# Pinning the loads of a background matrix-vector product in program order, and splitting eight stored operands at their reload instead of at their store

## The chip, the cores and the metric

The kernel runs on one core of one Trainium2 chip. The metric is the device time of one execution in microseconds. Three runs of the kernel before took 2257.85, 2253.43 and 2251.84 us, a median of 2253.43 us.

## What is computed

One layer of a decoder trunk on a sequence of 1024 tokens with 1024 channels, all in float32. Cut to what matters here:

```
mod = silu(c) @ w_ada + b_ada                       # 1024 -> 6 * 1024
shift1, scale1, gate1, shift2, scale2, gate2 = split(mod)
u = x * (1 + scale1) + shift1
hq, hf, hi, hg, rq, rk, rv, rg, ga, gb = split(u @ w_in)      # 1024 -> 12288
ya = hgrn2(hq, hf, hi, hg) @ w_pa
yb = retention(rq, rk, rv, rg, positions) @ w_pb              # rq, rk are rotated
y  = (sigmoid(ga) * ya + sigmoid(gb) * yb) @ w_o
x  = layer_norm(alpha * x + (1 + gate1) * y)
u  = x * (1 + scale2) + shift2
h  = square(relu(u @ w_up + b_up))                            # 1024 -> 4096
y  = h @ w_down + b_down
x  = layer_norm(alpha * x + (1 + gate2) * y)
```

Two pieces of this are touched: the part of `mod` that is not needed at once (gate2, gate1, scale2, shift2), and the operands made from `h` on their way from the up projection to the down projection.

## The kernel before

**Matrix products.** Each float32 operand is split in two parts, a rounded high part made by ScalarE (line 174) and the rest made by VectorE (line 175), and each product of 128 x 512 outputs is three matmuls (lines 179 to 181). Most of the big projections are done in 2 x 2 blocks with seven products in place of eight: a group of 256 output channels has the seven products A11, S1, S2, S4, S3, A12 and A22, each of 12 matmuls. S1 to S4 are sums and differences of weight blocks that VectorE makes (line 225) from two raw pieces of the weights; the pieces are loaded through SyncE's DMA queue (line 322, 512 KB each, four buffers), and split parts of weights have six buffers. `seven` (line 441) runs the groups. In each group VectorE adds three pairs of results out of PSUM (line 450). The product A22 of a group writes on into the PSUM bank X that the last of these adds has read, so TensorE can't begin it before that add is done.

**Where the order comes from.** The code is a trace in program order. A planner then orders the instructions of each engine by its own estimate of when each is ready, so an instruction with nothing to wait for can go far ahead of its place in the trace. The engines then run their streams in that order, and an instruction that waits holds up all behind it on its engine or queue. `keep_in_program_order` sets an edge from the instruction that was traced last on the same engine, so the pinned one comes after that one; the ones behind it stay free.

**The modulation in the background.** 24 groups of `w_in` (the gates hg, ga and rg, and rq and rk) are computed by `seven` in about 317 to 790 us. Beside the groups that are not rq or rk, the generator `ada_rest` (line 1192) does the rest of `mod` on VectorE: 64 parts of 256 rows by 256 columns of `w_ada`. Each part is one load of 256 KB on SyncE's queue (line 1202, tag adw, four buffers) and two steps on VectorE (lines 582 and 583). After four parts the column sum over the 128 partitions is finished by `ada_row` (line 1227): a load of the bias (line 1233), a split of the sum (lines 1234 and 1236), two small matmuls (lines 1239 and 1240), an add (line 1243) and a store. Before the change the load of part n + 2 was traced behind the steps of part n, nothing but the first step of a part and two VectorE instructions of `ada_row` was pinned, and the planner could issue a load as soon as one of the four buffers was free.

In a group with modulation the calls fall behind the products S1, S4 and A22. The first eight groups take 1, 2 and 2 parts at these places, the eight rg groups 1, 1 and 2. The rg groups alternate with rq and rk groups, which take none; there VectorE has twelve instructions of the rotation to do (lines 731 to 736).

**The operands of h.** For each of 16 groups j of the up projection, `use_square` (line 1527) makes seven operands (L11, L12, L22, S1, S2, S3, S4) that the down projection multiplies, and `keep_h` (line 1516) stores each in DRAM through GpSimd's queue. For the pairs (j, name) in `H_PARTS`, which are L22 and S3 of the groups 0 to 13, it first splits the operand in two parts and stores both (256 KB each). In `down_seven` (line 1572) such a pair is loaded as two parts through GpSimd's queue (line 1593); every other operand comes as one tile through SyncE's queue (line 1596, tag hr, four buffers) and is split then, beside the matmuls. Group 0 is computed by `up_plain` (line 1558), groups 1 to 15 by `seven`. The stages of the down projection run in the order L12 with L11, S1 with S2, S4, S3, L22.

Of the kernel before, what the change touches and what calls it, by code (L numbers as in the profile page):

```python
# [19 lines left out]
P = 128  # L20
T = 1024
D = 1024  # L22
# [4 lines left out]
FT = DFF // P  # L27
# [24 lines left out]

H_DEFER = 4

H_PARTS = [(j, name) for j in range(FT // 2 - 2) for name in ("L22", "S3")]


H_FILL = (0, 4, 3, 0, 3, 0, 2, 0, 1, 0, 2, 0, 1)
# [47 lines left out]
def drain(g):  # L106
    for _ in g:
        pass
# [20 lines left out]
class Trunk:  # L129
# [1062 lines left out]
    def ada_rest(self):  # L1192

        ap = self.aw
        parts = [(s, g, q) for s, g in ADA_ORDER for q in range(4)]
        loaded = {}

        def load(n):
            s, g, q = parts[n]
            c0 = s * D + 256 * g  # L1200
            t = loaded[n] = ap.tile([P, 2, 256], F32, tag="adw", bufs=4, name=self.uid("adw"))
            self.nc.sync.dma_start(t, self.i["w_ada"][256 * q:256 * q + 256, c0:c0 + 256].rearrange("(k p) c -> p k c", p=P))

        ones = ap.tile([P, 1], F32R, name="ones_r")
        self.nc.scalar.activation(ones, self.ones, AF.Copy)
        load(0)
        load(1)
        yield

        ends = iter(())  # L1210
        for n, (s, g, q) in enumerate(parts):
            if q == 0:
                acc = ap.tile([P, 256], F32, tag="adacc", bufs=2, name=self.uid("acc"))
            w = loaded.pop(n)
            for j in (0, 1):
                r = self.ada_step(acc, w[:, j], 2 * q + j, q + j == 0)
                if j == 0:
                    self.tc.keep_in_program_order(r)
            if n + 2 < len(parts):
                load(n + 2)  # L1220
            next(ends, None)
            if q == 3:
                ends = self.ada_row(acc, s, g, ones)
            yield
        drain(ends)

    def ada_row(self, acc, sec, g, ones):

        nc, ap = self.nc, self.aw
        pin = self.tc.keep_in_program_order  # L1230
        hi, lo = (ap.tile([P, 256], F32R, tag="ad" + e, bufs=1, name=self.uid("ad" + e)) for e in "hl")
        br = ap.tile([1, 256], F32, tag="brow", bufs=4, name=self.uid("brow"))
        nc.sync.dma_start(br, self.i["b_ada"][0:1, sec * D + 256 * g:sec * D + 256 * g + 256])
        nc.scalar.activation(hi, acc, AF.Copy)
        yield
        pin(nc.vector.tensor_tensor(lo, acc, hi.bitcast(F32), op=ALU.subtract))
        yield
        pr = self.ps("b", (1, 256))
        nc.tensor.matmul(pr, ones, hi, start=True, stop=False)
        nc.tensor.matmul(pr, ones, lo, start=False, stop=True)  # L1240
        yield
        plus = 0.0 if sec == S_SHIFT2 else 1.0
        pin(nc.vector.scalar_tensor_tensor(br, pr, plus, br, op0=ALU.add, op1=ALU.add))
        nc.gpsimd.dma_start(self.g_d[sec][0:1, 256 * g:256 * g + 256], br)
# [271 lines left out]
    def keep_h(self, j, name, t):  # L1516

        d = self.h_d[j][name]
        if (j, name) not in H_PARTS:
            self.nc.gpsimd.dma_start(d, t)  # L1520
# [37 lines left out]
    def up_plain(self):  # L1558
        wt = [self.W(("up", 0, t)) for t in (0, 1)]
        places = iter("grrrgrg")  # L1560
        tile = lambda: (self.tp.tile([P, 512], F32, tag="relu", bufs=4, name=self.uid("relu")) if next(places) == "r" else
                        self.wp.tile([P, 512], F32, tag="gate", bufs=2, name=self.uid("relu")))
        self.h_tile = lambda dt: self.tp.tile([P, 512], dt, tag="parts", bufs=4, name=self.uid("hp"))
        use = self.use_square(0, tile, (1, 1))
        for half in (0, 1):
            for m in (0, 1):
                use(m, half, self.dense_T(*wt[m], half), True)
                if (half, m) == (0, 0):
                    yield


    def down_seven(self):
# [25 lines left out]
        def prepare(n):  # L1598
# [25 lines left out]
            u = loaded.pop(n)  # L1624
            if (j, stages[s][p][0]) not in H_PARTS:
                hr, u = u, self.ut()
# [94 lines left out]
def build(ctx, tc, ins, out):  # L1721
# [13 lines left out]
    k.ga_d, k.gb_d, k.y1_d = dt("ga_d", KT), dt("gb_d", KT), dt("y1_d", KT)  # L1735
    k.h_d = [{c: [k.dp.tile([P, 512], F32R, name=f"h_d{j}{c}{e}") for e in "hl"] if (j, c) in H_PARTS else
              k.dp.tile([P, 512], F32, name=f"h_d{j}{c}") for c in ("L11", "L12", "L22", "S1", "S2", "S3", "S4")}
# [216 lines left out]
```

## Time and profile before

| | |
|---|---|
| median of three runs | 2253.43 us |
| the profiled execution: time, span | 2255.3 us, 2253.4 us |
| TensorE busy, granted clock over the span | 98%, 0.997 |
| VectorE, ScalarE, GpSimd busy | 75%, 45%, 15% |
| DMA traffic | 394.27 MB, mean 175 GB/s |
| 24 groups of `w_in` with the modulation beside them | about 317 to 790 us |
| up projection, groups 0 to 15 | about 1625 to 1945 us |
| down projection | about 1945 to 2245 us |

A line of a timeline gives the start and the duration in us, the engine (SPq is SyncE's DMA queue), the line of the code, the operation, output <- input, and in brackets the idle time just before it with what ended it. A line of the waits gives who waited, for whom, the sum in us, how often, and the longest. A line of the windows gives, for one stretch, the busy time of each engine with its count of instructions, then the granted TensorE clock, the DMA share and GB/s.

### The profile page before, as it was taken

The page shows a single profiled execution, that of the slowest core. Times are in us where ns is not written, and L with a number is a line of the kernel's source. Part 1 is how long each engine was busy: PE and PEld are TensorE (multiplying, and loading weights), DVE is VectorE, ACT ScalarE, POOL GpSimd, SP SyncE. Part 2 cuts the span into 40 slices and gives each one's busy share as a digit, 9 for nine tenths or more (in the row PEclk, how much of TensorE's full clock was granted, in tenths as well). Part 3 has the DMA queues.
Part 4 walks back from the last instruction along what each step waited for, and adds up shares of the span by engine and source line. Part 5 has one row for each costly group of instructions (what it writes and reads, how often), then busy time and mean ns, then how long its engine had stood idle before and what let it go on. Part 6 is the DMA issues. An engine that isn't in the chain of part 4 may idle for free.

```text
span 2253.4 us, 29560 instructions
## 1 busy us (share of the span) xinstructions
PE 2206.0 (98%) x10255; PEld 1830.1 (81%) x10255; DVE 1696.9 (75%) x3124; ACT 1005.7 (45%) x1726; POOL 333.7 (15%) x536
## 2 busy tenths in 40 slices
PE   6999999999999999999999999999999999999998
PEld 5888887887777788888878888888878888888886
DVE  7757777767777668888868778977796666559676
ACT  4533334433333334333366554453566666543520
POOL 0110111111110100001012221112112222100041
PEclk9999999999999999999999999999999999999999
DMA  9544645544343332213157667645345555678893
GB/s 309 188 162 161 208 151 175 187 139 140 112 136 113 126 103 76 75 57 113 52 201 242 206 217 268 216 158 183 113 162 183 182 182 182 230 269 298 292 302 126
DMA packets 239239, 394.27 MB, mean 175 GB/s; under 512 B 18272, under 2 KB 128624, under 8 KB 238832
## 3 DMA queue, kind: packets, MB, share of 16 engines
q1 hardware_dynamic: 196192, 276.53, 37.8%
q0 software_dynamic: 42576, 115.39, 14.8%
q8 instruction: 81, 1.33, 0.2%
q14 instruction: 70, 0.57, 0.1%
q10 hardware_dynamic: 320, 0.45, 0.1%
HBM read 287.43 MB, written 104.87 MB: 174 GB/s over the span
## 4 chain that ended last, share of the span: by engine, by line
PE 84%; DVE 8%; DMA 4%; issue 2%; ACT 1%; POOL 0%; ACTq 0%; DVEq 0%; SPq 0%; POOLq 0%
PE psd L179 15%; PE psd L180 15%; PE psd L181 15%; PE psa L181 5%; PE psa L179 5%; PE psa L180 5%; PE psc L181 3%; PE psc L179 3%; PE psc L180 3%; DMA raw<-in_w_in 2%; PE psb L179 2%; PE psb L180 2%; PE psb L181 2%; PE psa L852 1%; PE psc L852 1%
## 5 line engine op out<-in xcount | busy, mean ns | idle before, releaser
L179 PE MATMUL psd<-U,bh 128*128 128x512 f32 x616 | 241.7, 392 | 13.8 <-DVE e L450 11.9
L180 PE MATMUL psd<-U,bh 128*128 128x512 f32 x616 | 240.7, 391 | 0.0
L181 PE MATMUL psd<-U,bl 128*128 128x512 f32 x616 | 240.6, 391 | 0.0
L174 ACT ACTIVATE bh<-s 128x512 fp32r<-128x512 f32 x204 | 128.4, 630 | 233.2 <-PE psd L180 75.0
L179 PE MATMUL psd<-U,wh 128*128 128x512 f32 x504 | 202.5, 405 | 0.8 <-ACT U L174 0.8
L181 PE MATMUL psd<-U,wl 128*128 128x512 f32 x504 | 202.0, 401 | 0.0
L180 PE MATMUL psd<-U,wh 128*128 128x512 f32 x504 | 199.3, 395 | 2.3 <-DVE U L175 1.8
L174 ACT ACTIVATE bh<-raw 128x512 fp32r<-128x512 f32 x153 | 97.1, 638 | 195.0 <-PE psd L180 89.0
L175 DVE TENSOR_TENSOR bl<-raw,bh 128x512 fp32r<-128x512 f32 x153 | 104.4, 687 | 96.8 <-ACT bh L174 96.1
L175 DVE TENSOR_TENSOR bl<-s,bh 128x512 fp32r<-128x512 f32 x204 | 139.3, 684 | 43.5 <-ACT bh L174 43.1
L179 PEld LDWEIGHTS psd<-U,bh 128*128 128x128 f32 x616 | 116.0, 188 | 42.9 <-DVE e L450 14.8
L181 PEld LDWEIGHTS psd<-U,bl 128*128 128x128 f32 x616 | 116.1, 188 | 24.6
L180 PEld LDWEIGHTS psd<-U,bh 128*128 128x128 f32 x616 | 116.0, 188 | 23.7
L174 ACT ACTIVATE wh<-raw 128x512 fp32r<-128x512 f32 (+1 forms) x78 | 52.8, 695 | 165.1 <-PE psd L180 130.8
L181 PE MATMUL psa<-U,bl 128*128 128x512 f32 x312 | 121.7, 390 | 0.0
L180 PE MATMUL psa<-U,bh 128*128 128x512 f32 x312 | 121.5, 389 | 0.0
L179 PE MATMUL psa<-U,bh 128*128 128x512 f32 x312 | 121.5, 389 | 0.0
L180 PEld LDWEIGHTS psd<-U,wh 128*128 128x128 f32 x504 | 95.5, 189 | 23.5 <-DVE U L175 5.4
L179 PEld LDWEIGHTS psd<-U,wh 128*128 128x128 f32 x504 | 95.2, 190 | 19.4 <-ACT U L174 2.9
L181 PEld LDWEIGHTS psd<-U,wl 128*128 128x128 f32 x504 | 95.3, 189 | 18.9
L174 ACT ACTIVATE U<-hr 128x512 fp32r<-128x512 f32 x84 | 52.7, 628 | 84.4 <-PE psc L181 9.0
L175 DVE TENSOR_TENSOR wl<-raw,wh 128x512 fp32r<-128x512 f32 (+1 forms) x78 | 59.1, 769 | 36.0 <-ACT wh L174 33.3
(574 smaller groups left out, 5845.9 us busy)
## 6 DMA issues: line engine op xcount, KB each, us to landing
raw<-in_w_in SPq DMA_DIRECT2D x126, 512.0 KB, 4.4
raw<-in_w_down SPq DMA_DIRECT2D x64, 512.0 KB, 5.4
raw<-in_w_pb SPq DMA_DIRECT2D x36, 512.0 KB, 4.8
adw<-in_w_ada SPq DMA_DIRECT2D x64, 256.0 KB, 3.0
raw<-in_w_up SPq DMA_DIRECT2D x32, 512.0 KB, 3.7
adw<-in_w_ada SPq DMA_DIRECT2D x16, 512.0 KB, 7.8
rv_d<-e POOLq DMA_DIRECT2D x32, 256.0 KB, 3.9
rg_d<-e POOLq DMA_DIRECT2D x32, 256.0 KB, 2.4
```

Of the source, the lines that this page charges most:

```text
L174: pin(self.nc.scalar.activation(hi, src, AF.Copy))
L175: pin(self.nc.vector.tensor_tensor(lo, src, hi.bitcast(F32), op=ALU.subtract))
L179: r = mm(out, wh, uh, start=start, stop=False, skip_group_check=more)
L180: mm(out, wh, ul, start=False, stop=False, skip_group_check=more)
L181: return r, mm(out, wl, uh, start=False, stop=stop, skip_group_check=more)
L852: r = nc.tensor.matmul(ps[bk][:, c * 192:(c + 1) * 192].rearrange("p (b w r) -> p b w r", w=2, r=3 * sz), k[:, n * P:(n + 1) * P], mv, sta ...
```

## The change

1. Each load of a part of `w_ada` and each load of a bias row is pinned, and so are the second step of a part and the first of the two small matmuls. Three loads are traced at the start instead of two, and the load of part n + 3 instead of n + 2 stands behind the steps of part n.
2. `H_PARTS` begins at group 4 instead of 0: L22 and S3 of the groups 0 to 3 are stored as one tile each and are split when they come back in the down projection. The tile allocator for parts in `up_plain` (tag "parts", four buffers of 128 x 512) goes, since group 0 has no parts any more.

```diff
-H_PARTS = [(j, name) for j in range(FT // 2 - 2) for name in ("L22", "S3")]
+H_PARTS = [(j, name) for j in range(4, FT // 2 - 2) for name in ("L22", "S3")]
...
+        pin = self.tc.keep_in_program_order
 
         def load(n):
...
-            self.nc.sync.dma_start(t, self.i["w_ada"][256 * q:256 * q + 256, c0:c0 + 256].rearrange("(k p) c -> p k c", p=P))
+            pin(self.nc.sync.dma_start(t, self.i["w_ada"][256 * q:256 * q + 256, c0:c0 + 256].rearrange("(k p) c -> p k c", p=P)))
...
         load(0)
         load(1)
+        load(2)
         yield
...
             for j in (0, 1):
-                r = self.ada_step(acc, w[:, j], 2 * q + j, q + j == 0)
-                if j == 0:
-                    self.tc.keep_in_program_order(r)
-            if n + 2 < len(parts):
-                load(n + 2)
+                pin(self.ada_step(acc, w[:, j], 2 * q + j, q + j == 0))
+            if n + 3 < len(parts):
+                load(n + 3)
...
-        nc.sync.dma_start(br, self.i["b_ada"][0:1, sec * D + 256 * g:sec * D + 256 * g + 256])
+        pin(nc.sync.dma_start(br, self.i["b_ada"][0:1, sec * D + 256 * g:sec * D + 256 * g + 256]))
...
-        nc.tensor.matmul(pr, ones, hi, start=True, stop=False)
+        pin(nc.tensor.matmul(pr, ones, hi, start=True, stop=False))
         nc.tensor.matmul(pr, ones, lo, start=False, stop=True)
...
-        self.h_tile = lambda dt: self.tp.tile([P, 512], dt, tag="parts", bufs=4, name=self.uid("hp"))
```

## The prediction

> **What bounds the kernel now.** The page first: its table of engines.
>
> ```profile
> span 2253.4 us, 29560 instructions
> ## 1 busy us (share of the span) xinstructions
> PE 2206.0 (98%) x10255; PEld 1830.1 (81%) x10255; DVE 1696.9 (75%) x3124; ACT 1005.7 (45%) x1726; POOL 333.7 (15%) x536
> ```
>
> TensorE is the bound, and its matmuls stay as they are. What the change can win or lose is TensorE's idle time, 47 us in all, in the two places that it touches. So next the list of TensorE's waits over the whole run, and then the same list cut to 470 to 760 us (the third fence).
>
> ```profile
> PE psd L179 <- DVE e L450: 11.9, 7, 2.6
> ...
> PE psb L1240 <- DVE adl L1236: 2.7, 2, 1.5
> PE psd L179 <- ACT e L438: 1.9, 2, 1.2
> ...
> PE psc L179 <- ACT bh L174: 0.7, 1, 0.7
> ```
> ```profile
> PE psd L179 <- DVE e L450: 11.2, 6, 2.6
> ```
>
> The costliest wait is product A22 behind VectorE's add on its bank (L450). Six of its seven cases, 11.2 us, fall in the stage with the modulation; the seventh, 11.9 - 11.2 = 0.7 us, and the two waits for ScalarE (1.9 and 0.7) lie at the start of the up projection, 3.3 us together. Why the add is late I read in the timelines of SyncE's queue, VectorE and TensorE, around the longest case.
>
> ```profile
> 577.22 0.37 SPq L1202 DMA_DIRECT2D adw<-in_w_ada  x1
> 578.17 1.10 SPq L322 DMA_DIRECT2D raw<-in_w_in  x2
> ```
> ```profile
> 579.51 0.69 DVE L175 TENSOR_TENSOR bl<-s,bh 128x512 fp32r<-128x512 f32 x1 [0.80 <-ACT bh L174]
> 585.73 0.69 DVE L225 TENSOR_TENSOR s<-raw,raw 128x512 f32<-128x512 f32 x1 [5.52 <-DMA raw<-in_w_in]
> ```
> ```profile
> 589.74 0.64 PE L179 MATMUL psd<-U,bh 128*128 128x512 f32 x1 [2.60 <-DVE e L450]
> 590.17 0.63 PE L180 MATMUL psd<-U,bh 128*128 128x512 f32 x1
> ```
> ```profile
> 576.00:594.00 18.00, 15.40 (x62) 12.24 (x61) 10.76 (x20) 5.57 (x10) 2.15 (x4) 0.91 0.43 138
> ```
>
> VectorE stands 5.52 us at a sum of raw weights (L225) that isn't urgent, with the add queued behind it. The first of the two pieces, issued at 578.17, is in only at 585.73, 7.56 us later; the load of modulation weights went out 0.95 us ahead of it. Behind this stall the matmuls start 0.43 us apart, and the window shows the granted clock at 0.91: (1 - 0.91) x 18 = 1.6 us more. The first and the last of the six cases (piece, sum, product A22):
>
> ```profile
> 497.30 1.09 SPq L322 DMA_DIRECT2D raw<-in_w_in  x2
> 503.88 0.69 DVE L225 TENSOR_TENSOR s<-raw,raw 128x512 f32<-128x512 f32 x1 [4.55 <-DMA raw<-in_w_in]
> 507.89 0.50 PE L179 MATMUL psd<-U,bh 128*128 128x512 f32 x1 [1.64 <-DVE e L450]
> 702.21 1.10 SPq L322 DMA_DIRECT2D raw<-in_w_in  x2
> 708.74 0.69 DVE L225 TENSOR_TENSOR s<-raw,raw 128x512 f32<-128x512 f32 x1 [4.50 <-DMA raw<-in_w_in]
> 712.75 0.50 PE L179 MATMUL psd<-U,bh 128*128 128x512 f32 x1 [1.58 <-DVE e L450]
> ```
>
> From issue to use the piece takes 6.58 and 6.53 us here. TensorE's stall is this time less 4.94, 4.95 and 4.96 us in the three cases. So one rule holds for them: **stall = time of the piece - 4.95**. The mean stall of 11.2 / 6 = 1.87 us means a mean piece of 6.82 us.
>
> What would it be without the load ahead of it? By 742 us all modulation loads are done, and the same place of a group comes once more:
>
> ```profile
> 742.56 1.03 SPq L322 DMA_DIRECT2D raw<-in_w_in  x2
> 747.72 0.69 DVE L225 TENSOR_TENSOR s<-raw,raw 128x512 f32<-128x512 f32 x1 [3.13 <-DMA raw<-in_w_in]
> ```
>
> The piece takes 5.16 us, and by the rule TensorE would stall 0.21 us. The load ahead costs 6.82 - 5.16 = 1.66 us a case.
>
> **The change, part by part: the modulation.** A load is now pinned behind the SyncE instruction traced last. At the first call of an rg group (behind product S1) that is the second raw piece of the next group, traced while S1's weights were fetched. So the piece goes first, and the load stands behind it in the queue. It doesn't stand alone. Before, four buffers were refilled as each came free, and one load came due at this point. Now the load for part n + 3 has waited behind the piece, though its buffer was long free, and the load behind the next call needs the buffer of the part just used up, which is free too. So two loads of 256 KB leave right behind the piece and share the engines with it, and the other raw piece, which now leaves 0.6 us behind the first (two in 1.09 us), is pushed back by their two issues. The nearest rows are pieces in the groups between, with a load on their heels, and without:
>
> ```profile
> 515.10 0.37 SPq L322 DMA_DIRECT2D raw<-in_w_in  x1
> 515.56 0.46 SPq L1202 DMA_DIRECT2D adw<-in_w_ada  x1
> 519.63 0.69 DVE L225 TENSOR_TENSOR s<-raw,raw 128x512 f32<-128x512 f32 x1 [1.72 <-DMA raw<-in_w_in]
> 720.00 3.21 SPq L322 DMA_DIRECT2D raw<-in_w_in  x2
> 723.76 0.69 DVE L225 TENSOR_TENSOR s<-raw,raw 128x512 f32<-128x512 f32 x1 [0.94 <-DMA raw<-in_w_in]
> ```
>
> 4.53 against 3.76 us: 0.77 us for a load behind the piece. Two cost more, the other piece being later costs less; I take 0.77 for both together, between none (bound: 5.16) and the present 1.66 (bound: 6.82). Then the piece takes 5.93 us, the stall is 0.98, and six of them 5.9 us: **5.3 us won** (bounds 0 and 11.2 - 6 x 0.21 = 9.9). With stalls this short the dip of the clock goes, **1.6 us** (bounds 0 and 1.6): the stalls of 1.64 and 1.58 us are followed by a first matmul of 0.50 us, not 0.64. The clock's rule in the Trainium skill ("TensorE: Matmul & The Clock Gate", section "What's actually happening") is that it halves after an idle window of about 3.4 us. By that rule a stall of 2.60 us is too short to owe it the dip, and the sum would lack these 1.6 us; the trace, with 0.43 us between starts right behind the stall, speaks against it, and I keep them.
>
> The other pins. The second step of a part already hangs on the first, traced just before it on VectorE, so its pin changes nothing: 0. The bias load no longer runs ahead; nothing on TensorE waits for it: 0. The small matmul can't be issued before its place; the second one, which waits for VectorE, made both stalls of 2.7 us. The second of these (1.5) lies behind the stall at 747.72, which stays; I count 0 (bounds 0 and 2.7 won). On SyncE's queue raw pieces are issued behind loads that wait for a buffer, as before. The first load now leaves behind a raw piece instead of at the head of the stage; its first step is several microseconds further on, and VectorE can lose about 5.52 - 2.60 = 2.9 us before TensorE notices: 0.
>
> **The operands of h.** Two splits a group leave VectorE and ScalarE in the groups 0 to 3, and eight stores leave GpSimd's queue. VectorE at that time:
>
> ```profile
> 1652.02 0.68 DVE L175 TENSOR_TENSOR hp<-relu,hp 128x512 fp32r<-128x512 f32 x1
> 1652.62 0.68 DVE L1549 TENSOR_TENSOR relu<-relu,relu 128x512 f32<-128x512 f32 x1
> ```
> ```profile
> 1660.00:1670.00 10.00, 10.00 (x44) 8.16 (x45) 10.00 (x14) 7.50 (x12) 0.54 (x1) 1.00 0.25 81
> 1670.00:1680.00 10.00, 9.20 (x38) 6.55 (x37) 9.97 (x17) 7.97 (x14) 3.25 (x7) 1.00 0.53 151
> ```
> ```profile
> 1659.24 0.60 ACT L438 ACTIVATE e<-psd 128x512 f32<-128x512 f32 x1 [1.37 <-DMA h_d0S<-relu]
> ```
>
> VectorE is full (10.00 and 9.97 of 10 us) while TensorE stalls; the longest stall (1.2) stands behind ScalarE's wait for the store of group 0's last operand, which VectorE makes behind the splits. A split takes 0.60 us from start to start. Four of them, of the groups 0 and 1, lie ahead of the last stall: 4 x 0.60 = **2.4 us won**, out of 3.3 (bounds 1.2, if only group 0's count, and 3.3). Next late there is the raw weights' load again. The splits of the groups 2 and 3 lie behind the stalls: 0.
>
> They come back in the down projection: eight times
>
> ```profile
> L174 ACT ACTIVATE U<-hr x84: 612/632/660, 1921.3 to 2212.3; 128x512 fp32r<-128x512 f32 x84
> L175 DVE TENSOR_TENSOR U<-hr,U x84: 667/685/695, 1922.5 to 2215.7; 128x512 fp32r<-128x512 f32 x84
> ```
>
> Stage S3's four are made five products ahead, in 2130 to 2157 us, stage L22's in 2187 to 2200:
>
> ```profile
> 2143.00:2154.00 11.00, 11.00 (x50) 9.13 (x49) 0.69 (x1) 0.63 (x1) 4.23 (x8) 1.00 0.90 270
> 2187.00:2198.00 11.00, 11.00 (x50) 9.13 (x49) 7.76 (x13) 4.41 (x7) 5.30 (x11) 1.00 0.96 271
> ```
>
> VectorE has 10.3 and 3.2 us free there, and four splits need 2.7: 0, and 8 x 0.69 = 5.5 us if that cover were gone. Eight loads of one tile on SyncE's queue take the place of 16 on GpSimd's: 0.
>
> **The sum:** 5.3 + 1.6 + 2.4 = 9.3 us. The profiled execution took 2255.3 us, its span and 1.9 us around it; it would take 2246.0. It lies 1.9 us above the median of the runs, so the forecast for the median is 2253.4 - 9.3 = **2244.1 us**, in its own bounds 2241 to 2246.5. A measurement of this kernel tells about 0.3%, 6.8 us, from no change: faster means below 2246.7.
>
> **Rivals.** *Loads behind the piece cost it nothing.* Then each stall falls to 0.21 us: 9.9 + 1.6 + 2.4 = 13.9, 2239.5 us. For it: at 742 us the other raw piece follows by 0.6 us, and the first is still in 1.66 us sooner than with a load ahead. Against it: 4.53 against 3.76. The Trainium skill has this rule ("DMA: Bandwidth & Descriptors", section "Two DMAs through the same engine are not ordered"): in one queue of a DMA engine, descriptors start in order, though pipelined. The 0.77 us speak against it in part only, for there a load went ahead as well.
>
> *The pins do nothing for the time.* Two loads behind cost what one ahead did, 1.66 us. The stalls stay, and only the splits' 2.4 us are won: 2251.0 us. For it: twice the bytes, in the same few microseconds.
>
> *Slower: VectorE's order.* The planner places the sum L225 by its own estimate of the piece's landing. With the piece ahead in the queue it can put two more instructions of 0.60 us (a split and the next sum) ahead of the add. It decides where the piece still takes 6.82 us: each stall grows by 1.2, 6 x 1.2 = 7.2 us, and stalls above 2.6 us bring the clock's dip five times more, 8.0; less the splits' 2.4: 12.8 us slower, 2266 us. Against it: at 747.72, with no load on the queue, the sum stands at the same place.
>
> **Chances.** Forecast 0.42, nothing lost behind 0.18, pins idle 0.30, slower 0.10. Faster 0.42 + 0.18 = 0.60, same 0.30, slower 0.10. The range leaves out the slower case and the last of the deep one, and allows 2 us for the planner's new order elsewhere: 2237 to 2253.
>
> **What would show it.** In SyncE's timeline of an rg group, a raw piece ahead of two modulation loads; VectorE's stall at L225 near 3.9 us instead of 4.3 to 5.5; TensorE's waits for L450 near 6 us in that stage, and none with a clock below 1.00. At 1640 to 1700 us, waits of about 1 us instead of 3.3. In the down projection no wait, 92 splits of hr instead of 84. Wrong would be a piece of 6.8 us or more, a new TensorE wait on a VectorE step that waits for adw, or any wait of TensorE in 2110 to 2240 us.

## The result, and the profile after

The changed kernel takes 2235.18 us in the median of five runs (2234.24 to 2236.87); the kernel before took 2257.85 us beside it (2251.84 to 2258.61). The ratio is 0.991, 95% interval [0.9896, 0.9924]: faster by 0.8 to 1.0%. The forecast of 2244.1 us had the direction, but less than half of the gain, and the result lies 1.8 us below its range. The profiled executions differ by 2253.4 - 2234.6 = 18.8 us of span, the medians of this comparison by 22.7; the scatter of the kernel before from run to run (last section, 7 us) is wider than the 3.9 us between them. One run of 8403 us, of the kernel below that keeps no operand of h in two parts, is left out of all figures; the other four took 2237.0 to 2239.9 us.

The span and the table of engines of the changed kernel, from its page:

```profile
span 2234.6 us, 29509 instructions
## 1 busy us (share of the span) xinstructions
PE 2202.6 (99%) x10255; PEld 1829.7 (82%) x10255; DVE 1698.1 (76%) x3124; ACT 1006.1 (45%) x1726; POOL 322.0 (14%) x512
```

Where in the span the time went is read from three steps that both kernels take: the load of b_d behind the stage with the modulation, the last store of z_d ahead of the up projection, and the first store of the output. Timelines of SyncE's and GpSimd's queues, before and then after:

```profile
780.76 0.35 SPq L744 DMA_DIRECT2D U<-b_d  x1
1632.86 0.57 POOL L1502 DMA_DIRECT2D z_d<-zp  x1 [4.29 <-DVE zp L1501]
2233.22 17.32 SPq L1662 DMA_DIRECT2D out<-row  x8
```
```profile
766.02 0.35 SPq L745 DMA_DIRECT2D U<-b_d  x1
1618.37 0.57 POOL L1503 DMA_DIRECT2D z_d<-zp  x1 [4.29 <-DVE zp L1502]
2214.37 17.32 SPq L1662 DMA_DIRECT2D out<-row  x8
```

The stage with the modulation gave 780.76 - 766.02 = 14.7 us (forecast 6.9), the part from z_d to the output 600.4 - 596.0 = 4.4 us (forecast 2.4), and nothing else moved. The list of TensorE's waits after, cut to 470 to 760 us as before, and then three stretches of the windows:

```profile
PE psb L1241 <- DVE adl L1237: 1.0, 1, 1.0
PE psd L180 <- DVE e L451: 0.3, 1, 0.3
```
```profile
576.00:594.00 18.00, 18.00 (x82) 14.61 (x81) 12.98 (x24) 6.65 (x12) 1.65 (x3) 1.00 0.57 185
450.00:760.00 310.00, 308.73 (x1365) 252.56 (x1364) 240.24 (x416) 116.88 (x201) 38.53 (x72) 1.00 0.39 130
1640.00:1700.00 60.00, 59.96 (x263) 49.00 (x262) 49.97 (x75) 39.69 (x65) 11.91 (x22) 1.00 0.50 171
```

Of the 11.2 us behind VectorE's add, 0.3 are left, the clock stays at 1.00, and at the start of the up projection TensorE is busy for 59.96 of 60 us. The place that stalled longest before now looks like this, in the timelines of SyncE's queue and VectorE:

```profile
574.30 0.37 SPq L323 DMA_DIRECT2D raw<-in_w_in  x1
574.72 1.06 SPq L1204 DMA_DIRECT2D adw<-in_w_ada  x2
575.88 0.27 SPq L1234 DMA_DIRECT2D brow<-in_b_ada  x1
576.24 0.37 SPq L323 DMA_DIRECT2D raw<-in_w_in  x1
```
```profile
578.40 0.69 DVE L226 TENSOR_TENSOR s<-raw,raw 128x512 f32<-128x512 f32 x1 [2.07 <-DMA raw<-in_w_in]
579.01 0.68 DVE L451 TENSOR_TENSOR e<-psa,e 128x512 f32<-128x512 f32 x1
579.61 0.68 DVE L176 TENSOR_TENSOR bl<-s,bh 128x512 fp32r<-128x512 f32 x1
580.21 0.68 DVE L226 TENSOR_TENSOR s<-s,raw 128x512 f32<-128x512 f32 x1
```

The queue is as forecast: the piece, two modulation loads right behind it, and the next raw piece 1.94 us behind the first instead of 0.57 (before it started at 578.74, the first at 578.17). But the piece takes 4.10 us, not 5.93, and VectorE waits 2.07 us, not 3.9. The six pieces take 5.24, 4.10, 4.10, 4.97, 4.12 and 4.20 us, a mean of 4.46; VectorE's order behind the sum is the old one. The first and the fourth take 0.8 to 1.1 us more than the rest, though the next raw piece leaves 2.8 and 3.4 us behind them; with narrow loads (below) the fourth still takes 4.93, and no run shows why. The longest still shows in TensorE:

```profile
496.82 0.37 SPq L323 DMA_DIRECT2D raw<-in_w_in  x1
...
502.06 0.69 DVE L226 TENSOR_TENSOR s<-raw,raw 128x512 f32<-128x512 f32 x1 [3.21 <-DMA raw<-in_w_in]
```

5.24 - 4.95 = 0.29 us is the whole of the 0.3 above.

**What a wait really costs.** The list of waits is shorter than the loss. TensorE's timeline of the kernel before around the stall of 1.58 us at 712.75:

```profile
710.56 0.39 PE L180 MATMUL psc<-U,bh 128*128 128x512 f32 x1
710.78 0.39 PE L181 MATMUL psc<-U,bl 128*128 128x512 f32 x1
...
713.09 0.40 PE L180 MATMUL psd<-U,bh 128*128 128x512 f32 x1
713.33 0.40 PE L181 MATMUL psd<-U,bl 128*128 128x512 f32 x1
```

In full work matmuls start 0.23 us apart, and each is on record for 0.39, since they overlap; idle time is counted only from the end of that. From 710.78 to 712.75 are 1.97 us, 1.74 more than 0.23; the next start comes after 0.34, 0.11 more. So a listed wait of 1.58 us costs 1.85: **0.27 us on top of each stall**. Added up over all starts from 300 to 775 us, the time lost this way is 17.5 us before (six stalls 12.7, the dip of the clock 1.7, small matmuls 3.05) and 2.4 after (0.8, 0, 1.5).

### The profile page after: what moved, and what is told of

It is laid out like the page before. It is cut to its first block, busy times and chain, and to the rows that moved or that the text cites. A ratio compares the mean times of both kernels' runs of the same rounds, so it can differ in the third digit from the quotient of the medians.

```text
span 2234.6 us, 29509 instructions
## 1 busy us (share of the span) xinstructions
PE 2202.6 (99%) x10255; PEld 1829.7 (82%) x10255; DVE 1698.1 (76%) x3124; ACT 1006.1 (45%) x1726; POOL 322.0 (14%) x512
## 4 chain that ended last, share of the span: by engine, by line
PE 92%; DVE 4%; DMA 1%; issue 1%; ACT 1%; POOL 0%; ACTq 0%; DVEq 0%; POOLq 0%; SPq 0%
PE psd L181 16%; PE psd L182 16%; PE psd L180 16%; PE psa L181 5%; PE psa L180 5%; PE psa L182 5%; PE psc L182 4%; PE psc L180 4%; PE psc L181 4%; PE psb L180 2%; PE psb L181 2%; PE psb L182 2%; PE psa L853 1%; PE psc L853 1%; PE psc L1151 1%
## 5 line engine op out<-in xcount | busy, mean ns | idle before, releaser
L180 PEld LDWEIGHTS psd<-U,wh 128*128 128x128 f32 x504 | 94.9, 189 | 19.9 <-ACT U L175 3.4
L182 PEld LDWEIGHTS psd<-U,wl 128*128 128x128 f32 x504 | 95.4, 189 | 18.8
L175 ACT ACTIVATE U<-hr 128x512 fp32r<-128x512 f32 x92 | 57.7, 628 | 103.6 <-issue 14.9
L176 DVE TENSOR_TENSOR U<-hr,U 128x512 fp32r<-128x512 f32 x92 | 63.1, 688 | 50.1 <-ACT U L175 44.3
```

The costliest lines, as they stand in the source:

```text
L175: pin(self.nc.scalar.activation(hi, src, AF.Copy))
L176: pin(self.nc.vector.tensor_tensor(lo, src, hi.bitcast(F32), op=ALU.subtract))
L180: r = mm(out, wh, uh, start=start, stop=False, skip_group_check=more)
L182: return r, mm(out, wl, uh, start=False, stop=stop, skip_group_check=more)
```

## Experiments

**One part at a time.** The modulation alone (H_PARTS and the tile for parts as before):

```
-H_PARTS = [(j, name) for j in range(4, FT // 2 - 2) for name in ("L22", "S3")]
+H_PARTS = [(j, name) for j in range(FT // 2 - 2) for name in ("L22", "S3")]
```

> The pins and the third load ahead are made; the operands of h are kept as before. Theory A (the trace of the two kernels): the stage with the modulation alone gave the 14.4 to 14.7 us by which its end moved, so this kernel lies about 14.5 us below the kernel before. Theory B (the sums of the forecast): 5.3 + 1.6 = 6.9 us below, and the rest of the gain comes from the operands of h or from the two together. If A holds, the raw pieces of the rg groups take 4.1 to 5.2 us from issue to sum, and product A22 waits for VectorE less than 1 us in all there.

Measured: 2239.6 us beside 2255.71 before, ratio 0.9924 [0.9912, 0.9937], 16.1 us. The pieces take 4.69, 3.98, 4.16, 4.68, 4.07 and 3.98 us, no stall of product A22 is left, and the time lost from 300 to 775 us is 1.7. Theory A; the forecast's 6.9 is out.

The operands of h alone, the same edit the other way in the kernel before:

> Only the operands of h are changed, the modulation is as before. Theory A (the trace): the end of the up projection moved 4.3 us more than its start did, so this kernel lies about 4.3 us below the kernel before, with the six stalls behind VectorE's add still there (11 us). Theory B (the forecast): 2.4 us below. If the tile that went away (the buffers of the parts) mattered for the modulation too, more than 6 us.

Measured: 2251.94 us beside 2255.71, ratio 0.9983 [0.9974, 0.9992], so 1.8 to 5.9 us, 3.8 in the middle. Theory A, though the interval holds 2.4 too; the traces decide, for from the last z_d to the output it takes 596.0 us here as in the changed kernel, and 600.5 in the kernel with the modulation alone. The two parts add up: 16.1 + 3.8 = 19.9 us, where both together, with two loads ahead (next run), gave 20.2 on the same chip. The six stalls are there as before:

```profile
PE psd L179 <- DVE e L450: 9.8, 6, 2.2
PE psb L1240 <- DVE adl L1236: 1.2, 1, 1.2
```

**Which of the pins, and how deep.** Two loads ahead in the changed kernel:

```
-        load(2)
...
-            if n + 3 < len(parts):
-                load(n + 3)
+            if n + 2 < len(parts):
+                load(n + 2)
```

> The changed kernel with two modulation loads ahead, as before, in place of three; all pins stay. Theory A (the pins put the loads behind the raw piece, the depth doesn't matter): within 2 us of the changed kernel, 17 to 19 us below the kernel before. Rival (the third load ahead is needed, for a pinned load leaves late and its step then waits for it): VectorE's waits for the modulation weights appear, and 4 to 8 us of the gain are lost.

Measured: 2235.53 us, ratio 0.9911 [0.9898, 0.9925], as the changed kernel. The third load ahead is worth nothing.

No pin on the loads of w_ada, all else as changed (`pin(self.nc.sync.dma_start(t, ...))` without the pin):

> The changed kernel without the pin on the loads of the modulation weights; the pins on steps, bias load and small matmul stay, and three ahead. Theory A (it is the loads' pin): the loads leave ahead of the raw piece again, the piece takes about 6.5 us, and 7 to 14 us of the gain are lost. Rival (the pins on the steps or the third load ahead do it): it stays within 2 us of the changed kernel.

Measured: 2244.42 us (2241.09 to 2249.91), ratio 0.9958 [0.9944, 0.9971]; 8.9 us of the gain are lost beside the kernel with two loads ahead, measured on the same chip. Theory A. SyncE's queue, VectorE and TensorE at the fourth of the six places:

```profile
613.27 0.37 SPq L1204 DMA_DIRECT2D adw<-in_w_ada  x1
613.75 0.26 SPq L1234 DMA_DIRECT2D brow<-in_b_ada  x1
614.23 1.11 SPq L323 DMA_DIRECT2D raw<-in_w_in  x2
```
```profile
617.87 0.69 DVE L451 TENSOR_TENSOR e<-psa,e 128x512 f32<-128x512 f32 x1 [1.60 <-PE psa L182]
618.47 0.68 DVE L176 TENSOR_TENSOR bl<-s,bh 128x512 fp32r<-128x512 f32 x1
621.58 0.69 DVE L226 TENSOR_TENSOR s<-raw,raw 128x512 f32<-128x512 f32 x1 [2.42 <-DMA raw<-in_w_in]
```

The load is ahead again and the piece takes 7.35 us (mean of six 6.62). But here the planner has put the sum two instructions later, behind the add on psa and a split, which stood behind it in the kernel before and in the changed one. Less is then left between the sum and the add that TensorE needs, and the stall is the piece's time less 5.76, not less 4.95: 1.59 us here, 5.2 in all.

The loads' pin alone, with the operands of h as changed (no other pin, two ahead):

```
-            self.nc.sync.dma_start(t, self.i["w_ada"][...])
+            self.tc.keep_in_program_order(self.nc.sync.dma_start(t, self.i["w_ada"][...]))
```

> The kernel before with two edits alone: the loads of the modulation weights are pinned (two ahead, as before), and the operands of h are kept in two parts from group 4 on. No pin on the second steps, the bias load and the small matmul. Theory A (of the pins only that on the loads moves the time): within 1.5 us of the changed kernel, with raw pieces of 4 to 5 us and no stall of product A22 above 0.4 us. Rival (the small matmul's or the steps' pins give a part): the waits of the small matmul are at 2.7 us again, not 1.2, and 1.5 to 3 us of the gain are missing.

Measured: 2235.36 us beside 2258.59, ratio 0.9897 [0.988, 0.9913]. Theory A: one pin is the whole gain of this stage, within the scatter. The pieces take 3.94 to 4.84 us, and of the small matmul's waits 1.1 us is left without its pin, as with it (1.0 and, at about 350 us, 0.2):

```profile
PE psb L1240 <- DVE adl L1236: 1.1, 1, 1.1
```

**Why the piece got so short.** Two things change for it at once: no load ahead, and the next raw piece pushed back by what now lies between. Narrow loads take the bytes away and leave every issue in place (edit of both kernels; `ada_step` reads the 32 columns eight times):

```
-            ...dma_start(t, self.i["w_ada"][256 * q:256 * q + 256, c0:c0 + 256]...
+            ...dma_start(t[:, :, :32], self.i["w_ada"][256 * q:256 * q + 256, c0:c0 + 32]...
```

> The kernel before, with the same narrow loads (32 of 256 columns, the modulation not computed), still ahead of the raw piece. Theory A (the bytes of the load ahead hold the piece up): the piece falls from 6.8 to the 5.2 us of the place with no load ahead, TensorE's stalls from 11.2 us to about 1.3, and the kernel lies 11 to 12 us below the kernel before. Rival (it is the order in the queue, a transfer ahead costs about the same whatever its size): pieces stay above 6 us, and the time stays within 3 us of the kernel before.

Measured: 2239.6 us beside 2255.22, ratio 0.9932 [0.9918, 0.9946]. Theory A, though the piece fell further than it said, and 15.6 us came instead of 11 to 12: less than it said is left of the stalls, and the 0.27 us per stall and the small matmul were not in the sum.

```profile
649.35 0.37 SPq L1204 DMA_DIRECT2D adw<-in_w_ada  x1
650.31 0.98 SPq L322 DMA_DIRECT2D raw<-in_w_in  x2
```
```profile
654.38 0.69 DVE L225 TENSOR_TENSOR s<-raw,raw 128x512 f32<-128x512 f32 x1 [2.03 <-DMA raw<-in_w_in]
```

With 32 KB ahead the piece takes 4.07 us here, 4.67 in the mean: **256 KB ahead cost 6.82 - 4.67 = 2.15 us**.

> The changed kernel, but each load of modulation weights fetches 32 of its 256 columns (32 KB in place of 256 KB), and the steps read these 32 columns eight times: the modulation is not computed, all instructions and their order stay. What do two loads behind a raw piece cost it? Theory A (the next raw piece, 512 KB, close behind is what lengthens a piece, the small loads only push it back): the piece of the steady groups stays at about 4.1 us. Theory B (the bytes of the two loads still cost some): it falls towards the 3.5 to 3.8 us of a piece with nothing behind it. The time stays within 2 us of the changed kernel by both, for no piece there delays TensorE by more than 0.3 us.

Measured: 2234.27 us, ratio 0.991 [0.9896, 0.9923], no change in the time. The four steady pieces (all but the first and the fourth) take 3.58, 3.67, 3.75 and 3.78 us, in place of 4.10, 4.10, 4.12 and 4.20: theory B, **two loads behind cost 0.43 us**.

The next raw piece pushed back in the kernel before, the load still ahead (three loads of 256 bytes behind the second piece of a group):

```
+        if getattr(self, "aw", None) is not None and i % 2 == 1:
+            pin = self.tc.keep_in_program_order
+            for _ in range(3):
+                z = self.aw.tile([1, 64], F32, tag="gap", bufs=4, name=self.uid("gap"))
+                pin(self.nc.sync.dma_start(z, self.i["b_ada"][0:1, 0:64]))
```

> The kernel before, with three loads of 256 bytes pinned between a raw piece and the next one in the rg groups, so that the next piece leaves about 1.5 to 2 us behind in place of 0.64; the modulation load stays ahead. Theory A (the next piece close behind costs 1 us or more of the piece's time): the piece falls from 6.8 to 5.4 to 5.9 us, the stalls from 11.2 to 3 to 6 us, and the kernel lies 5 to 9 us below the kernel before. Rival (only the load ahead costs): pieces stay at 6.5 to 6.8, no gain.

Measured: 2248.46 us beside 2255.22, ratio 0.9976 [0.9964, 0.9988], 6.8 us. At the third place:

```profile
574.69 0.37 SPq L1207 DMA_DIRECT2D adw<-in_w_ada  x1
575.65 0.37 SPq L322 DMA_DIRECT2D raw<-in_w_in  x1
576.07 1.12 SPq L328 DMA_DIRECT2D gap<-in_b_ada  x3
577.29 0.39 SPq L322 DMA_DIRECT2D raw<-in_w_in  x1
```
```profile
581.88 0.69 DVE L225 TENSOR_TENSOR s<-raw,raw 128x512 f32<-128x512 f32 x1 [4.19 <-DMA raw<-in_w_in]
```
```profile
585.89 0.50 PE L179 MATMUL psd<-U,bh 128*128 128x512 f32 x1 [1.27 <-DVE e L455]
```

The next piece leaves 1.64 us behind, and the piece takes 6.23 (mean of six 6.04, stalls 6.5 us in all): pushing it back by 1.1 us gives **0.78 us**. Theory A in kind, but the piece and the stalls fell a little less than it said. The three prices close the account: 6.82 - 2.15 + 0.43 - 4.46 = 0.64 us is left for the next piece's place in the changed kernel, and 4.67 - 4.00 = 0.67 between the two kernels with narrow loads (means of six). These two rest on much the same rows; the 0.78 here is the independent figure beside them.

**More bytes, ahead and behind.** Each load followed by 128 KB that nothing reads:

```
+            x = ap.tile([P, 2, 128], F32, tag="adx", bufs=3, name=self.uid("adx"))
+            pin(self.nc.sync.dma_start(x, self.i["w_ada"][256 * q:256 * q + 256, c0:c0 + 128]...
```

> The kernel before, with 128 KB more fetched behind each modulation load (half of it again, into a tile that nothing reads), so 384 KB ahead of the raw piece in place of 256. Here the planner puts the sum of raw weights two steps later, as where the loads were not pinned, so the slack is 5.76 us in place of 4.95. Theory A (bytes ahead in the queue cost a piece their own time: 2.15 us for 256 KB by the narrow loads): the piece takes about 6.82 + 1.08 = 7.9 us, the stalls 2.1 us each, 13 us in all. Rival (only the fact of a load ahead counts): pieces stay near 6.6 us, as with loads that were not pinned, and the stalls near 5 us in all.

Measured: 2259.53 us beside 2255.8, ratio 1.0014 [1.0004, 1.0024]. The pieces take 7.28 us in the mean, 0.46 more than the 6.82 of the kernel before, and 0.67 more than the 6.62 of the kernel with the loads not pinned, which has the same order of VectorE and 256 KB ahead. That is between the theories: bytes ahead cost, but 0.46 to 0.67 us for 128 KB where A said 1.08. Stalls are 10.0 us in all.

> The changed kernel with the same 128 KB more behind each modulation load, so 768 KB behind the raw piece ahead of the next one in place of 512, in four issues. VectorE's order stays. Theory A (bytes behind cost a piece little, and push the next piece further back): the steady pieces stay at 3.9 to 4.4 us, and the time within 2 us of the changed kernel. Rival (bytes behind cost as much as bytes ahead): 2.15 us for each 256 KB, so pieces of 6 us and more, and stalls of 1 us each.

Measured: 2236.22 us, ratio 0.991 [0.9894, 0.9927]. The last of the six, with four issues between the pieces:

```profile
689.83 0.37 SPq L323 DMA_DIRECT2D raw<-in_w_in  x1
...
692.82 0.37 SPq L323 DMA_DIRECT2D raw<-in_w_in  x1
```
```profile
693.97 0.69 DVE L226 TENSOR_TENSOR s<-raw,raw 128x512 f32<-128x512 f32 x1 [2.11 <-DMA raw<-in_w_in]
```

4.14 us with 768 KB behind, the mean of six 4.28: no more than with 512. Theory A. The next raw piece leaves 2.99 us behind here instead of 1.94, so this is the net of more bytes and a later neighbour. 128 KB more ahead lengthened the piece by 0.46 to 0.67 us.

**The operands of h.** Only the groups 0 and 1 left out:

```
-H_PARTS = [(j, name) for j in range(4, FT // 2 - 2) for name in ("L22", "S3")]
+H_PARTS = [(j, name) for j in range(2, FT // 2 - 2) for name in ("L22", "S3")]
```

> The changed kernel with the operands of h kept in two parts from group 2 on, not from group 4 on: only the groups 0 and 1 are left out. Theory A (the forecast's step: only the splits of the groups 0 and 1 lie ahead of the last stall, those of the groups 2 and 3 cost nothing): within 1 us of the changed kernel, and the stalls at the start of the up projection stay away. Rival (VectorE is full there for longer, and each split left out counts): part of the stalls is back, 1 to 3 us slower than the changed kernel.

Measured: 2234.79 us, ratio 0.9904 [0.9889, 0.9919], and no wait of TensorE from 1640 to 1900 us. Theory A. Neither this kernel nor any other in this section is faster than the changed one by more than the scatter.

None kept in two parts (`H_PARTS = []`):

> The changed kernel with no operand of h kept in two parts: 20 more splits move to the down projection, 112 in all. Theory A (the forecast's cover: VectorE and ScalarE have room in the last two stages): no wait of TensorE in the down projection, within 2 us of the changed kernel. Rival (VectorE runs out: 20 x 0.69 us on top, most of it in stage S3 and L22, where TensorE takes 1.3 to 2.6 us a product): TensorE waits for VectorE's splits there, and the kernel is 3 to 14 us slower than the changed one.

Measured: ratio 0.9928 [0.9914, 0.9942], 16 us below the kernel before, and from the last z_d to the output 600.5 us, 4.5 more than in the changed kernel. That is the rival, at the low end of its range: the forecast's cover holds for 8 splits and not for 28. The waits of TensorE from 1630 to 2230 us, and a window:

```profile
PE psd L180 <- DVE row L1668: 1.9, 1, 1.9
PE psd L180 <- ACT e L439: 0.4, 1, 0.4
```
```profile
2150.00:2182.00 32.00, 30.45 (x135) 24.88 (x133) 32.00 (x60) 15.23 (x26) 3.91 (x4) 1.00 0.65 208
```

VectorE is busy for all of the 32 us, with splits for the stages S3 and L22 among its work, and its add of the bank psd onto the rows (L1668) comes late. The stall of 1.9 us and a dip of the clock behind it make up most of the 4.5.

## Why the prediction was right or wrong

The direction and the mechanism were right: the modulation load went out behind the piece, the stalls behind VectorE's add all but vanished, and the clock stayed up. The size was wrong by 9 us. The step that failed is the time of the piece and with it the term of 5.3 us; three smaller terms were short too.

- **"Then the piece takes 5.93 us" failed.** It is 4.46. The base of 5.16 was one row, with the next piece 0.57 us behind, and a high one: in the thirteen other traces the piece at this place, at about 730 to 750 us, takes 4.53 to 4.86 us (4.68 to 4.84 in the three where the next piece follows as close), and by the narrow loads a piece with nothing big ahead takes 4.67. And the 0.77 us set on top for the two loads behind came from a row with another load ahead of it in the stage; they cost 0.43, and give back 0.6 to 0.8 because their issues keep the next 512 KB off. That "the other piece being later costs less" stood in the text, and it was the larger of the two. So the six waits gave 10.9 us, not 5.3. The rival *loads behind the piece cost it nothing* came nearest with 2239.5 us; its reason holds only in part, since they do cost something.
- **The rule stall = piece - 4.95 held** (0.29 at 5.24 us, 1.27 at 6.23 with the gap), as long as VectorE's order stands. What a stall costs is 0.27 us more than its listed wait, and neither the six stalls nor the four at the start of the up projection had that in the sum: 2.1 us (1.0 of the former, with what little is left after, and 1.1 of the latter).
- **The small matmul, counted 0**, gave 1.5 us (3.05 lost before, 1.5 after), inside its bounds. Its pin is not the cause, but mostly the loads' pin: the first wait, at about 350 us, is 1.1 us before and 1.1 with every pin but that on the loads, 0.2 in the changed kernel, and gone with the loads' pin alone. The second, behind 730 us, fell from 1.5 to 1.0 us; it is 1.2 in the kernel with only the operands of h changed, so much of that is scatter.
- **The splits, 2.4 of 3.3 us**: all 3.3 went, and with 4 x 0.27 us that is the 4.4 measured. That only the groups 0 and 1 count was right. The four terms come to 5.6 + 2.1 + 1.5 + 0.9 = 10.1 us, where the spans fell by 9.5 more than forecast.

Right in size were the dip of the clock (1.6 us), and the terms at zero. That there was one dip to win was luck of the profiled execution: the kernel with only the operands of h changed has the same six stalls and two dips. The zeros are the second step, the bias load, the third load ahead, and the down projection, where TensorE has no wait from 1900 us on. The splits there, from the page:

```profile
L175 ACT ACTIVATE U<-hr 128x512 fp32r<-128x512 f32 x92 | 57.7, 628 | 103.6 <-issue 14.9
L176 DVE TENSOR_TENSOR U<-hr,U 128x512 fp32r<-128x512 f32 x92 | 63.1, 688 | 50.1 <-ACT U L175 44.3
```

*Slower: VectorE's order* was wrong in sign too. Where the planner did move the sum two places back, without the loads' pin, the stall grew shorter by 0.81 us, since the two instructions moved out from between the late sum and the urgent add. *The pins do nothing* is out, since the pin on the loads alone gave the whole gain of its stage.

## What to carry to other kernels

When a waiting instruction holds up an urgent one, look at what was issued ahead of its transfer and close behind it: here a background load that ran ahead of an urgent piece on the same queue cost it several times what it cost from behind (2.15 us for one, 0.43 for two), and there it even served as a spacer. Price such a stall by the distance between the starts of the matmuls around it rather than by the listed wait, and take the undisturbed time of a transfer from several places, not from one row. Work moved under the cover of another stage is free only up to what the busiest stretch of that stage has left.

## What the runs showed of the hardware that was not expected

**Order in one queue.** 256 KB issued 0.96 us ahead of a 512 KB piece lengthen it by 2.15 us, 512 KB issued right behind by 0.43, and another 512 KB piece 0.57 us behind, in place of 1.6 to 1.9, by 0.64 to 0.78. With 768 KB right behind, and the next piece 2.99 us off, the piece was no longer than with 512. The Trainium skill ("DMA: Bandwidth & Descriptors", section "Two DMAs through the same engine are not ordered") says that the descriptors of one queue of a DMA engine start in order and are pipelined; the large price ahead and the small one behind agree with it.

**The clock.** It dipped not by the length of the stall alone. With 384 KB ahead, TensorE's timeline behind a stall of 2.39 us:

```profile
673.59 0.80 PE L179 MATMUL psd<-U,bh 128*128 128x512 f32 x1 [2.39 <-DVE e L450]
674.18 0.63 PE L180 MATMUL psd<-U,bh 128*128 128x512 f32 x1
674.61 0.63 PE L181 MATMUL psd<-U,bl 128*128 128x512 f32 x1
```

The starts are 0.43 us apart, for about 3.2 us. The same followed a stall of 1.94 us in that kernel and one of 1.91 with no parts, and did not follow stalls of 2.22 us (before) and 2.25 (384 KB ahead). The Trainium skill ("TensorE: Matmul & The Clock Gate", section "What's actually happening") gives a free-running window of about 3.4 us, with the clock halved after an idle one. The length of the dip and its hit or miss agree with such a window; that a whole window must be idle doesn't, for stalls of 1.91 and 1.94 us were enough.

The traces show what decides. In the two stretches named below every dip of the fourteen traces lasts 3.41 us, and it begins a whole number of steps of 3.413 us after the first dip of its trace, which comes at 35 to 38 us. On that grid, windows of the kernel before around its stalls of 2.60 and 2.22 us:

```profile
586.53:589.94 3.41, 0.81 (x4) 0.39 (x3) 3.41 (x7) 1.37 (x3) 0.56 (x1) 1.00 0.01 2
589.94:593.36 3.42, 3.42 (x9) 2.64 (x9) 3.15 (x6) 0.93 (x2) 0.55 (x1) 0.50 0.50 161
630.90:634.32 3.42, 2.04 (x9) 1.70 (x10) 3.42 (x7) 1.16 (x2) 0.76 (x2) 1.00 0.32 105
```

The stall of 2.60 us lies in one window, which leaves TensorE 0.81 us of work, and the next window runs at half clock. The stall of 2.22 us is cut by the edge at 630.90 into 0.85 and 1.37 us, and no dip follows. Added up over the distances between starts, in the stretches from 300 to 786 and from 1620 to 2216 us of all fourteen traces, the seven windows ahead of a dip had lost 2.08 to 2.76 us, and no other window at full clock more than 2.01. So in these traces about 60% of one window lost, in one stall or in several, halves the clock in the next, and where a stall falls on the grid decides as much as its length. The rule is read from the traces; no run varied it by itself.

**The scatter.** Kernels with the six stalls scatter over 6 to 9 us from run to run (the kernel before 2251.8 to 2258.6, the one without the loads' pin 2241.1 to 2249.9), the changed one over less than 3 (2234.2 to 2236.9). The kernel with the modulation alone, which keeps the waits at the start of the up projection and had a dip behind them, scatters over 6.6 (2234.2 to 2240.8). That each stall is as long as a transfer takes, and that some bring a dip and some don't, would make it so; no run shows it apart.
